# A two-layer hybrid trunk on one core: each GLA head's diagonal and smallest-block products come one projection product later, and layer 0's output projection takes K in another order

## The chip, the cores and the metric

The kernel runs on one core of a Trainium2 chip. The metric is the device time of one execution in microseconds, the median of several runs. A core has five engines with instruction streams of their own that meet only at semaphores: TensorE (PE; its weight loads are shown as PEld), VectorE (DVE), ScalarE (ACT), GpSimd (POOL) and SyncE (SP), which here issues the large weight loads as DMAs. Each engine takes its instructions strictly in the order in which they stand in its stream.

## What is computed

Two decoder layers on 512 tokens of width 1024. Layer 0 mixes by sliding-window attention and a short gated convolution, layer 1 by gated linear attention (GLA). A convolution MLP and a gated embedding follow in each. The two places that the change touches:

```python
def _attn_conv_mixer(h, ...):                      # layer 0
    ...
    return jnp.concatenate([attn, conv], axis=-1) @ w_out      # K = 512 attention + 512 convolution

def _gla_chunked(q, k, v, log_a):                  # layer 1, four heads, chunks of 64
    def step(state, inp):
        ...
        decay = jnp.exp(jnp.where(causal[:, :, None], rel, -jnp.inf))
        scores = jnp.einsum('bhtd,bhsd,bhtsd->bhts', qi, ki, decay)
        o_intra = jnp.einsum('bhts,bhsv->bhtv', scores, vi)
        state = jnp.exp(g_end)[..., None] * state + jnp.einsum(
            'bhsd,bhsv->bhdv', ki * jnp.exp(g_end[:, :, None, :] - gi), vi)
        return state, o_inter + o_intra
```

## The kernel before

Activations lie with features on the 128 partitions and the 512 tokens along the free axis. Almost all the work is products in fp32 precision made of three products of split operands (`mm3`, lines 157 to 159): the high half of the weight times the high half of the activation, high times low, low times high. Each weight block is loaded by SP into a buffer "raw" (two of them), ACT rounds it to the high half "wh" (line 137) and DVE subtracts that to make the low half "wl" (line 138).

**Layer 0's output projection** (`project`, line 348, with the `load` of line 745) goes through four blocks of 256 output columns. In each it loads all 1024 rows of K, and each of two output tiles sums 8 K tiles, 24 products. The K tiles are `ya + yc`: four attention tiles first, written by `mix` (line 640; its product is line 647, and ACT and DVE split it at lines 101 and 102), then four convolution tiles, of which `conv_out(0)` made two much earlier and `conv_out(1)` the other two just before. The attention rows of the weight are loaded by two DMAs for 64 partitions each, the convolution rows by one.

**GLA's heads** (`mixer1`, line 1472). While TensorE runs the layer's input projections (queries, keys, values and gates, in fp32r products of three), the intra-chunk scores of the four heads are worked out between them. A score block of 128x128 is cut into levels: at level b the lower-left blocks of b tokens in blocks of 2b are a product of two factors that carry the decay to the middle of the block. For each head h:

- `base(h)`: the running sum G of the log decays (DVE scan, line 1603); the factor of the diagonal, k times q at even tokens (line 1610); the sum over features of that factor by a product with ones (TensorE, line 1612); its placing on the even diagonal of the scores "sc" (DVE, line 1614, which reads the product from PSUM).
- `decay(h, levels)`: for each level, two differences of G (lines 1627, 1629), the exponential on ACT (1630; 1632 and 1633 at level 64) and the products with k and q (1634, 1635). `lo` is levels 64, 32, 16 and 8, `hi` is level 4.
- `level(h, levels)`: the products (lines 1648 and 1651) and their placing in sc (1659, 1661).
- `decay_pairs(h)` and `level_pairs(h)`: levels 2 and 1, with factors made in place in k and q (line 1676 on DVE, line 1678 on ACT), one set of products (1686) and four masked copies by DVE (1692, 1697).
- `decay_off`, `off`, `state`, `read`, `turn`: the part between chunks (transposes at 1730, states at 1743 and 1745), the output (1766, 1768, 1770, 1775) and its transposes (1782, 1786).

`query`, `key` and `gate` (lines 1520, 1526, 1531) are one projection product each, 24 products of 128x512. `Values.step(i)` is half of a value projection, 48 products of 128x336, whose sums ACT writes to vt (line 1505). The order of these calls at the end of `mixer1` (lines 1789 to 1889) is written out by hand; within it a scheduler places each engine's instructions, by priorities that follow the order of the calls.

Four PSUM buffers "ps" hold projection sums and four "pa" all other products. SBUF tiles with the tag "F" (the diagonal's factor, the levels' factors, the states' factors) share eight slots.

Of the kernel before, what the change touches and what calls it, by code (L numbers as in the profile page):

```python
# [18 lines left out]
P = 128  # L19
S = 512  # L20
# [36 lines left out]
class Kernel:  # L57
# [366 lines left out]
    def mixer0(self):  # L424
        nc, a, tc = self.nc, self.a, self.tc
        with tc.tile_pool(name="m0", bufs=1) as mp:
# [68 lines left out]
            h = HD // 2  # L495
# [161 lines left out]
            yc = [None] * 4  # L657
# [87 lines left out]
        def load(raw, cols):  # L745
            w = a["hy_w_out"][0]
            for g in range(2):
                nc.sync.dma_start(
                    raw[64 * g : 64 * g + 64, :4, :],
                    w[256 * g : 256 * g + 256, cols].rearrange("(j p) n -> p j n", p=64),  # L750
                )
            nc.sync.dma_start(raw[:, 4:, :], w[512:, cols].rearrange("(k p) n -> p k n", p=P))

        return lambda done, then: self.project(load, ya + yc, done, then)


    def operand(self, m, gain, tags):
# [714 lines left out]
    def mixer1(self):  # L1472
# [4 lines left out]
        with tc.tile_pool(name="m1", bufs=1) as mp:  # L1477
# [31 lines left out]
            def pair_w(c0):  # L1509
                return self.weights(w_in[:, :, c0 : c0 + 256], ND, 256)  # L1510
# [7 lines left out]
            def query(w, h):  # L1518
                o = qT[h] = self.fp.tile([P, S], F32, tag="a0", name=self.nm("qT"))
                nc.vector.scalar_tensor_tensor(  # L1520
                    out=o, in0=feature(w, h % 2), scalar=float(GDK**-0.5), in1=R, op0=ALU.mult, op1=ALU.mult
                )

            def key(w, h):
                o = kT[h] = self.fp.tile([P, S], F32, tag="a0", name=self.nm("kT"))
                nc.vector.tensor_tensor(o, feature(w, h % 2), R, ALU.mult)
# [70 lines left out]
            second = lambda x, b: x.rearrange("p (n b) -> p n b", b=2 * b)[:, :, b:]  # L1597
            scores, Gs, Fs = {}, {}, {}

            def base(h):  # L1600

                G = Gs[h] = mp.tile([P, S], F32, tag="G", name=self.nm("G"), bufs=2)
                nc.vector.tensor_tensor_scan(
                    G, run.rearrange("p a b -> p (a b)"), las[h], 0.0, op0=ALU.mult, op1=ALU.add
                )
                sc = scores[h] = mp.tile([P, GDV * NT], F32, tag="sc", name=self.nm("sc"), bufs=3)

                pr = new()[:, : S // 2]
                ev = lambda x: x.rearrange("p (n b) -> p n b", b=2)[:, :, 0]
                nc.vector.tensor_tensor(pr, ev(kT[h]), ev(qT[h]), ALU.mult)  # L1610
                pd = self.pa()[:, : S // 2]
                mm(pd, self.ones, pr, start=True, stop=True)
                nc.gpsimd.memset(sc[:, :S], 0.0)
                nc.vector.tensor_tensor(
                    sc[:, :S].rearrange("p (a n b) -> p a n b", a=NT, b=2)[:, :, :, 0],
                    pd.rearrange("p (a n) -> p a n", a=NT),
                    ev(self.ident).unsqueeze(1).to_broadcast([P, NT, P // 2]), ALU.mult,
                )
# [18 lines left out]
            def level(h, levels):  # L1637
                A = scores[h][:, :S]
                for l in levels:
                    b, F = LEVELS[l], Fs[h, l]  # L1640
                    pl = self.pa()
                    for t in range(NT):
                        c = slice(t * P, (t + 1) * P)
                        if b < 64:

                            for u in (0, 64):
                                d = slice(t * P + u, t * P + u + 64)
                                mm(second(pl[u : u + 64, d], b), F[:, d], second(F[:, d], b), start=True, stop=True)
                        else:
                            mid = t * P + b  # L1650
                            mm(pl[:b, mid : mid + b], F[:, t * P : mid], F[:, mid : mid + b], start=True, stop=True)
                    if b < 64:
                        for u in (0, 64):
                            r = slice(u, u + 64)
                            tv = lambda x: x.rearrange("p (t c) -> p t c", c=P)[r, :, r].rearrange(
                                "p t (n b) -> p t n b", b=2 * b
                            )[:, :, :, b:]
                            mk = second(msk[r, l, r], b).unsqueeze(1).to_broadcast([64, NT, 32 // b, b])
                            nc.vector.copy_predicated(tv(A), mk, tv(pl))
                    else:  # L1660
                        nc.vector.tensor_copy(second(A[:b], b), second(pl[:b], b))
# [18 lines left out]
            def level_pairs(h):  # L1680

                A = scores[h][:, :S]
                pl = self.pa()
                for d0 in range(0, S, 64):
                    d, u = slice(d0, d0 + 64), d0 % P
                    mm(pl[u : u + 64, d], kT[h][:, d], qT[h][:, d], start=True, stop=True)
                two, one = LEVELS.index(2), LEVELS.index(1)
                for u in (0, 64):
                    r = slice(u, u + 64)
                    v4 = lambda x: x.rearrange("p (t c) -> p t c", c=P)[r, :, r].rearrange("p t (n b) -> p t n b", b=4)  # L1690
                    m = msk[r, two, r].rearrange("p (n b) -> p n b", b=4)[:, :, 2:]
                    nc.vector.copy_predicated(
                        v4(A)[:, :, :, 2:], m.unsqueeze(1).to_broadcast([64, NT, 16, 2]), v4(pl)[:, :, :, 0:4:2]
                    )
                    v2 = lambda x: x.rearrange("p (t c) -> p t c", c=P)[r, :, r].rearrange("p t (n b) -> p t n b", b=2)
                    m = msk[r, one, r].rearrange("p (n b) -> p n b", b=2)[:, :, 1]
                    nc.vector.copy_predicated(
                        v2(A)[:, :, :, 1], m.unsqueeze(1).to_broadcast([64, NT, 32]), v2(pl)[:, :, :, 1]
                    )
# [111 lines left out]
            base(0)  # L1811
            decay(0, lo)
            query(w, 2)
            level(0, lo)
            decay(0, hi)
            decay_off(0)
# [1 line left out]
            query(w, 3)  # L1818
            w = pair_w(768)
            level(0, hi)  # L1820
            level_pairs(0)
            off(0)
            base(1)
            decay(1, lo)
            key(w, 2)
            key(w, 3)
            v = Values(0, 336, 336)
            level(1, lo)
# [2 lines left out]
            decay_pairs(1)  # L1831
            v.step(0)
            level(1, hi)
            level_pairs(1)
            off(1)
            base(2)
            decay(2, lo)
            v.step(1)
            v = Values(336, 672, 336)
            state(0)  # L1840
            level(2, lo)
            read(0)
# [2 lines left out]
            decay_pairs(2)  # L1845
            v.step(0)
            level(2, hi)
            level_pairs(2)
            off(2)
            turn(0)  # L1850
            base(3)
            decay(3, lo)
            v.step(1)
            w = pair_w(2064)
            state(1)
            level(3, lo)
            read(1)
# [7 lines left out]
            w = pair_w(2064 + 256)  # L1865
            self.load_vectors_ffn(1)
            level(3, hi)
            level_pairs(3)
            off(3)
            read(2)  # L1870
            gate(w, 2)
            turn(2)
            state(3)
# [54 lines left out]
```

## Time and profile before

| what | value |
|---|---|
| median of 3 runs | 1230.61 us (1229.55 to 1232.44) |
| the profiled execution | 1231.84 us |
| its span in the trace | 1230.1 us |
| TensorE's granted clock, mean | 0.999 |
| HBM traffic | 114.37 MB read, 2.10 MB written |

Line numbers (L137) are those of the kernel before. A row of the timeline gives start, duration, engine, line, operation, what it writes and reads, how many follow each other, and in brackets how long the engine sat idle before it and what ended that. Matmuls are pipelined: one starts before the one ahead of it has ended, so durations overlap and a wait is better measured from start to start. A row of the chain of waits gives start, duration and instruction. A row of the windows gives the stretch, its length, the busy time and number of instructions of PE, PEld, DVE, ACT and POOL, the clock, the busy share of the DMA engines and GB/s. A row of TensorE's waits gives what waited for whom, the total in us, how many times and the longest.

### The profile page before, as it was taken

What the parts mean: (1) busy time and instruction counts of PE and PEld (TensorE: products, weight loads), DVE (VectorE), ACT (ScalarE), POOL (GpSimd) and SP (SyncE); (2) the same over time, 40 slices, a digit from 0 to 9 for tenths busy, and PEclk for the clock granted to TensorE, in tenths of its full rate; (3) what the DMA queues carried; (4) which work ended last, traced back from release to release, by engine and by line L of the source; (5) the groups of instructions that cost most, each with busy time, mean ns of one, the idle gap of its engine ahead of it and who ended that gap; (6) DMA issues with size and microseconds to landing.
All of it is one profiled execution on the core that took longest, in us unless ns stands there. A gap on an engine that the chain in (4) does not pass through costs nothing.

```text
span 1230.1 us, 17710 instructions
## 1 busy us (share of the span) xinstructions
PE 1218.1 (99%) x7028; PEld 1053.8 (86%) x7028; DVE 969.7 (79%) x1537; ACT 665.7 (54%) x1084; POOL 43.7 (4%) x64
## 2 busy tenths in 40 slices
PE   9999999999999999999999999999999999999998
PEld 8877789989899889888987888889998989889887
DVE  6886587899898986746679875677999888987595
ACT  7466455656555644534563554555555555645374
POOL 2500000000000000000100000000000000000000
PEclk9999999999999999999999999999999999999999
DMA  7221322423233232222322222313242322422501
GB/s 217 87 88 46 86 78 69 137 69 116 91 103 103 93 130 95 94 91 88 112 91 68 70 69 69 103 42 130 69 137 69 121 85 95 146 95 95 205 2 69
DMA packets 111063, 117.61 MB, mean 96 GB/s; under 512 B 2776, under 2 KB 106258, under 8 KB 110980
## 3 DMA queue, kind: packets, MB, share of 16 engines
q1 hardware_dynamic: 109616, 115.35, 28.4%
q8 instruction: 55, 0.90, 0.3%
q0 software_dynamic: 560, 0.42, 0.3%
q10 hardware_dynamic: 804, 0.70, 0.2%
q14 instruction: 28, 0.23, 0.1%
HBM read 114.37 MB, written 2.10 MB: 95 GB/s over the span
## 4 chain that ended last, share of the span: by engine, by line
PE 79%; DVE 13%; ACT 3%; issue 2%; DMA 1%; POOL 1%; ACTq 0%; DVEq 0%; POOLq 0%
PE ps L157 12%; PE ps L158 11%; PE ps L159 11%; PE pa L158 6%; PE pa L157 6%; PE pa L159 6%; PE ps L847 5%; PE ps L845 5%; PE ps L846 5%; PE pa L847 2%; PE pa L846 2%; PE pa L845 2%; DVE wl L138 2%; DVE zt L905 1%; DMA raw<-in_ffn_w_up_dram 1%
## 5 line engine op out<-in xcount | busy, mean ns | idle before, releaser
L137 ACT ACTIVATE wh<-raw 128x1024 fp32r<-128x1024 f32 (+4 forms) x154 | 152.2, 991 | 159.0 <-PE ps L158 114.3
L138 DVE TENSOR_TENSOR wl<-raw,wh 128x1024 fp32r<-128x1024 f32 (+4 forms) x154 | 175.3, 1139 | 50.6 <-ACT wh L137 48.6
L793 ACT ACTIVATE wh<-raw 128x1024 fp32r<-128x1024 f32 x78 | 82.3, 1056 | 114.0 <-DVE raw L818 66.1
L905 DVE SCALAR_TENSOR_TENSOR zt<-z,vfa,zt 128x510 f32<-128x510 f32 (+1 forms) x176 | 131.2, 747 | 9.6 <-ACT zt L903 8.9
L794 DVE TENSOR_TENSOR wl<-raw,wh 128x1024 fp32r<-128x1024 f32 x78 | 95.4, 1223 | 14.8 <-ACT wh L793 14.7
L903 ACT ACTIVATE zt<-z,vfb 128x512 f32<-128x512 f32 x88 | 70.6, 809 | 16.4 <-DVE z L896 4.9
L157 PE MATMUL ps<-b,wh 128*128 128x512 f32 x192 | 76.2, 398 | 0.7 <-ACT b L101 0.5
L159 PE MATMUL ps<-b,wl 128*128 128x512 f32 x192 | 75.9, 396 | 0.0
L158 PE MATMUL ps<-b,wh 128*128 128x512 f32 x192 | 75.1, 392 | 0.0
L157 PE MATMUL pa<-a,wh 128*128 128x512 f32 x176 | 69.0, 392 | 0.0
L157 PE MATMUL pa<-b,wh 128*128 128x512 f32 x176 | 69.0, 392 | 0.0
L158 PE MATMUL pa<-a,wh 128*128 128x512 f32 x176 | 69.0, 392 | 0.0
L158 PE MATMUL pa<-b,wh 128*128 128x512 f32 x176 | 69.0, 392 | 0.0
L159 PE MATMUL pa<-a,wl 128*128 128x512 f32 x176 | 68.6, 390 | 0.1
L159 PE MATMUL pa<-b,wl 128*128 128x512 f32 x176 | 68.5, 389 | 0.0
L847 PE MATMUL ps<-four,wl 128*128 128x256 f32 x232 | 65.7, 283 | 0.0
L846 PE MATMUL ps<-four,wh 128*128 128x256 f32 x232 | 65.6, 283 | 0.0
L845 PE MATMUL ps<-four,wh 128*128 128x256 f32 x232 | 65.6, 283 | 0.0
L157 PE MATMUL ps<-a,wh 128*128 128x512 f32 x160 | 63.1, 394 | 0.0
L158 PE MATMUL ps<-a,wh 128*128 128x512 f32 x160 | 62.5, 391 | 0.0
L159 PE MATMUL ps<-a,wl 128*128 128x512 f32 x160 | 62.4, 390 | 0.0
L157 PE MATMUL ps<-uh,wh 128*128 128x512 f32 x128 | 50.3, 393 | 0.0
(470 smaller groups left out, 3527.4 us busy)
## 6 DMA issues: line engine op xcount, KB each, us to landing
raw<-in_ffn_w_up_dram SPq DMA_DIRECT2D x44, 1024.0 KB, 5.0
raw<-in_ffn_w_down_dram SPq DMA_DIRECT2D x13, 1024.0 KB, 4.7
raw<-in_hy_w_in_dram SPq DMA_DIRECT2D x8, 1024.0 KB, 4.9
raw<-in_gla_w_in_dram SPq DMA_DIRECT2D x8, 1024.0 KB, 5.1
raw<-in_ffn_w_down_dram SPq DMA_DIRECT2D x8, 768.0 KB, 4.3
raw<-in_ple_w_gate_dram SPq DMA_DIRECT2D x6, 1024.0 KB, 4.6
raw<-in_gla_w_out_dram SPq DMA_DIRECT2D x4, 1024.0 KB, 4.7
zt<-in_ffn_w_down_dram SPq DMA_DIRECT2D x6, 512.0 KB, 3.4
```

Source lines behind the costliest of these rows:

```text
L137: nc.scalar.activation(hv, v, AF.Copy)
L138: nc.vector.tensor_tensor(lv, v, hv.bitcast(F32), ALU.subtract)
L157: mm(out, lh, rh, start=start, stop=False, **kw)
L158: mm(out, lh, rl, start=False, stop=False, **kw)
L159: mm(out, ll, rh, start=False, stop=stop, **kw)
L793: nc.scalar.activation(h, src, AF.Copy)
L794: nc.vector.tensor_tensor(l, src, h.bitcast(F32), ALU.subtract)
L845: mm(out, wh, xh, start=first and j == 0, stop=False, **kw)
L846: mm(out, wh, xl, start=False, stop=False, **kw)
L847: mm(out, wl, xh, start=False, stop=j == ND // 2 - 1, **kw)
L903: nc.scalar.activation(y, z, AF.Identity, scale=w2[:, f : f + 1], bias=bb[:, f : f + 1])
L905: nc.vector.scalar_tensor_tensor(out=y[:, tap:], in0=z[:, : S - tap], scalar=w[:, f : f + 1], in1=y[:, tap:], op0=ALU.mult, op1=ALU.add,)
```

## The change

Two edits. First, in layer 0's output projection the order over K becomes convolution tiles 0 and 1, attention tiles 0 to 3, convolution tiles 2 and 3. The weight rows go to the matching places of the buffer, and the convolution rows come in two DMAs instead of one:

```diff
                 nc.sync.dma_start(
-                    raw[64 * g : 64 * g + 64, :4, :],
+                    raw[64 * g : 64 * g + 64, 2:6, :],
                     w[256 * g : 256 * g + 256, cols].rearrange("(j p) n -> p j n", p=64),
                 )
-            nc.sync.dma_start(raw[:, 4:, :], w[512:, cols].rearrange("(k p) n -> p k n", p=P))
-
-        return lambda done, then: self.project(load, ya + yc, done, then)
+            for k, r in ((0, 512), (6, 768)):
+                nc.sync.dma_start(raw[:, k : k + 2, :], w[r : r + 256, cols].rearrange("(k p) n -> p k n", p=P))
+
+
+        ys = yc[:2] + ya + yc[2:]
+        return lambda done, then: self.project(load, ys, done, then)
```

Second, `base(h)` keeps the scan, the diagonal's factor and the clearing of sc, and its product with ones and the placing become a function `diag(h)`, called one projection product later. `level_pairs(h)` is called one projection product later too:

```diff
-                pr = new()[:, : S // 2]
-                ev = lambda x: x.rearrange("p (n b) -> p n b", b=2)[:, :, 0]
+                pr = Fs[h, "diag"] = new()[:, : S // 2]
                 nc.vector.tensor_tensor(pr, ev(kT[h]), ev(qT[h]), ALU.mult)
+                nc.gpsimd.memset(sc[:, :S], 0.0)
+
+            def diag(h):
+                sc = scores[h]
                 pd = self.pa()[:, : S // 2]
-                mm(pd, self.ones, pr, start=True, stop=True)
-                nc.gpsimd.memset(sc[:, :S], 0.0)
+                mm(pd, self.ones, Fs[h, "diag"], start=True, stop=True)
                 nc.vector.tensor_tensor(
...
             query(w, 2)
+            diag(0)
             level(0, lo)
...
             level(0, hi)
-            level_pairs(0)
             off(0)
             base(1)
             decay(1, lo)
             key(w, 2)
+            level_pairs(0)
+            diag(1)
             key(w, 3)
...
             level(1, hi)
-            level_pairs(1)
             off(1)
             base(2)
             decay(2, lo)
             v.step(1)
             v = Values(336, 672, 336)
+            level_pairs(1)
+            diag(2)
             state(0)
...
             level(2, hi)
-            level_pairs(2)
             off(2)
             turn(0)
             base(3)
             decay(3, lo)
             v.step(1)
             w = pair_w(2064)
+            level_pairs(2)
+            diag(3)
             state(1)
...
             level(3, hi)
-            level_pairs(3)
             off(3)
             read(2)
+            level_pairs(3)
             gate(w, 2)
```

The number of instructions on TensorE, DVE, ACT and POOL stays the same; SP issues four DMAs more.

More of the change, by code (lines that the diff above doesn't have):

```diff
@@ L1598, in mixer1 @@
             scores, Gs, Fs = {}, {}, {}
+            ev = lambda x: x.rearrange("p (n b) -> p n b", b=2)[:, :, 0]
             def base(h):
```

## The prediction

> **What bounds the kernel now.** I read the page first, then TensorE's waits, the chain of waits and the two stages that the diff touches.
>
> ```profile
> span 1230.1 us, 17710 instructions
> ...
> PE 1218.1 (99%) x7028; PEld 1053.8 (86%) x7028; DVE 969.7 (79%) x1537; ACT 665.7 (54%) x1084; POOL 43.7 (4%) x64
> ```
> ```profile
> PE pa L1612 <- DVE F L1610: 1.5, 2, 1.0
> PE pa L1686 <- ACT qT L1678: 1.3, 2, 0.7
> ...
> PE ps L157 <- ACT b L101: 0.5, 1, 0.5
> ```
>
> TensorE is busy for 1218.1 of 1230.1 us, so the kernel is a string of products and an edit that adds or drops none can gain only where TensorE stands still: 12.0 us in all. Of its waits the diff aims at three: the diagonal product (L1612) for its factor from DVE, the smallest-block products (L1686) for qT from ACT, and layer 0's output projection (L157) for a split by ACT. Two things follow. The gain is a few us at most, and it holds only if no other engine is the limit in that place. That needs the windows and the chain in the GLA heads.
>
> ```profile
> 630.00:684.00 54.00, 51.50 (x403) 43.97 (x401) 52.68 (x126) 24.20 (x46) 0.00 (x0) 1.00 0.17 52
> ```
> ```profile
> 630.05 1.23 DVE wl L138
> ...
> 681.54 0.34 DVE F L1629
> ```
>
> From 630 to 684 us (columns: PE, weight loads, DVE, ACT, POOL) DVE is busy for 52.68 of 54.00 us, more than PE's 51.50, and the chain of work that ended last runs along DVE from 630.05 to 681.54, with one ACT step in between. So in heads 0 to 2 DVE sets the pace, and this change takes no DVE work away. It lets TensorE do other products meanwhile. The gain is the sum of TensorE's waits that vanish less those that DVE brings back elsewhere. The clock column is 1.00: it plays no part.
>
> **Part 1, layer 0's output projection.** All its products are kept; the order over K becomes two convolution tiles, the four attention tiles, the other two convolution tiles.
>
> ```profile
> 138.02 1.94 PE L647 MATMUL pa<-pT,v 128*64 128x512 f32 x8
> 140.43 0.98 PE L157 MATMUL ps<-b,wh 128*128 128x512 f32 x3 [0.46 <-ACT b L101]
> ...
> 142.63 0.40 PE L157 MATMUL ps<-b,wh 128*128 128x512 f32 x1
> ```
> ```profile
> 140.12 0.26 ACT L101 ACTIVATE b<-pa 128x128 fp32r<-128x128 f32 x1
> ...
> 142.35 0.28 ACT L101 ACTIVATE b<-pa 128x128 fp32r<-128x128 f32 x1 [0.36 <-DVE b L102]
> ```
> ```profile
> 142.66 0.29 DVE L102 TENSOR_TENSOR b<-pa,b 128x128 fp32r<-128x128 f32 x1 [0.34 <-ACT b L101]
> ```
>
> The attention product ends at 139.96 and the projection waits 0.46 us for the first split. A product of 0.39 us is followed after 0.227 (24 of them in 5.45), so 0.16 us of overlap is lost too. The nine products from 140.43 to 142.63 take 2.20 where nine at 0.227 take 2.04: another 0.16. The two convolution tiles were ready long before, so the whole **0.8 us** goes. Their six products take 1.36 us and end near 141.0; the attention splits run from 140.12 to 142.95, each needed 0.68 us after the one before, and the last low half (142.95) is needed near 143.2. That is a margin of 0.2 to 0.3. If the splits come later than that, the wait comes back there: 0 to 0.8 us.
>
> The weight load becomes four transfers instead of three (a 512 KB one is split), so SP's queue gets four more issues, one in each load; behind them stand only later weight loads, which wait for their buffers. POOL's queue keeps its order.
>
> ```profile
> raw<-in_hy_w_out_dram SPq DMA_DIRECT2D x8, 256.0 KB, 3.8
> raw<-in_hy_w_out_dram SPq DMA_DIRECT2D x4, 512.0 KB, 5.0
> ```
> ```profile
> 146.76 1.06 ACT L137 ACTIVATE wh<-raw 128x1024 fp32r<-128x1024 f32 x1 [4.12 <-PE ps L158]
> ```
>
> ACT starts on the next block at 146.76 because TensorE frees a buffer, not because data land, and it had stood idle for 4.12 us. Four more issues, one to each of the four loads, hide there: nothing. Without that cover each could cost at most its own 3.8 us. The Trainium skill (DMA: Bandwidth & Descriptors, Rules for kernel authors) speaks against this piece: it wants transfers of 1 MiB or more and advises against splitting. Its fit of about 2.0 us fixed cost for each would make an estimated 8 us for four loads if they were on the path; by the wait above they are not, and the measured 3.8 and 5.0 us decide.
>
> **Part 2, the heads.** Each head's L1612 (with its DVE reader L1614) and L1686 (with two L1692 and two L1697) move behind one more projection product. Every fp32 product is two rows of the trace. On DVE the four copies (about 0.45 us each, 1.8) now come after the next head's scan (L1603) and factor (L1610), which so start 1.8 us sooner; the copies' reader, the head's read, comes many us later. The last head's L1686 goes in among the products of read(2); it waited for nothing and I cost that move at nothing.
>
> ```profile
> 648.25 0.66 PE L1648 MATMUL pa<-F 128*64 128x32 f32 x16
> 649.53 0.69 PE L1686 MATMUL pa<-qT,kT 128*64 128x64 f32 x16 [0.61 <-ACT qT L1678]
> ...
> 654.19 0.67 PE L1612 MATMUL pa<-F,ones 128*128 128x256 f32 x2 [0.98 <-DVE F L1610]
> ...
> 672.73 0.66 PE L1648 MATMUL pa<-F 128*64 128x32 f32 x16
> 674.12 0.69 PE L1686 MATMUL pa<-qT,kT 128*64 128x64 f32 x16 [0.73 <-ACT qT L1678]
> ...
> 683.12 0.60 PE L1743 MATMUL pa<-vt,F 128*128 128x256 f32 x2
> 683.89 0.70 PE L1743 MATMUL pa<-vt,F 128*128 128x256 f32 x2 [0.17 <-ACT vt L1505]
> ...
> 698.72 0.66 PE L1648 MATMUL pa<-F 128*64 128x32 f32 x16
> 699.20 0.66 PE L1686 MATMUL pa<-qT,kT 128*64 128x64 f32 x16
> ...
> 702.98 0.67 PE L1612 MATMUL pa<-F,ones 128*128 128x256 f32 x2 [0.53 <-DVE F L1610]
> ```
>
> Undisturbed, L1686 starts 0.48 us after L1648 (698.72 to 699.20). In head 0 it took 1.28, in head 1 1.39: **0.80** and **0.91** us lost. The diagonals of heads 1 and 3 lose **0.98** and **0.53**; those of heads 0 and 2 wait for nothing. In head 2 the moved products also fill the **0.17** that L1743 waits for vt. Together 3.39 us; with part 1, 4.19.
>
> The Trainium skill (Trainium Kernel Development and Optimization, Performance Expectations) calls matmul busy time a bad metric, since matmuls are pipelined. By idle time alone, 0.61 and 0.73 in place of 0.80 and 0.91 and 0.46 in place of 0.8, the sum would be 0.71 less; I go by starts, as these rows allow.
>
> What comes back, **head 0**: the diagonal now stands right before the level products. PSUM's "pa" has four buffers, and diagonal, levels 64, 32, 16 and 8 need five, so the fifth waits until L1614 has read the diagonal. In the changed instruction lists L1614 stands behind qT's L1520.
>
> ```profile
> 641.09 1.57 PE L1648 MATMUL pa<-F 128*64 128x32 f32 x47
> ```
> ```profile
> 636.99 0.42 DVE L1614 TENSOR_TENSOR sc<-pa,cf 128x256 f32<-128x256 f32 x1
> 637.32 0.42 DVE L1629 TENSOR_TENSOR F<-G 128x256 f32<-128x256 f32 x1
> ...
> 642.28 0.70 DVE L1520 SCALAR_TENSOR_TENSOR qT<-ps,R 128x512 f32<-128x512 f32 x1
> 642.88 0.42 DVE L1661 COPY sc<-pa 64x256 f32<-64x256 f32 x1
> ```
>
> Taking L1614 and one more 0.33 us instruction away ahead of L1520 and putting one of 0.27 there brings L1520 to 641.9 and L1614 to 642.5, done at 642.9. TensorE reaches the last third of these rows at 641.09 + 2/3 of 1.5 = 642.1. So it waits about **0.85** us, and the level products, query(3) and SP's later loads stand behind it. Bounds: 0, and 1.7 if L1614 comes twice as late.
>
> **Head 1** has DVE's whole load behind it, so what TensorE wins must not run into it. The nearest place is the fourth "ps" bank of the value product, which key(3)'s L1526 frees:
>
> ```profile
> 664.58 0.67 DVE L1526 TENSOR_TENSOR kT<-ps,R 128x512 f32<-128x512 f32 x1
> ```
> ```profile
> 666.65 0.32 PE L157 MATMUL ps<-wh,b 128*128 128x336 f32 x1
> ```
>
> TensorE comes there at 666.65 less 0.80 and 0.98 plus 0.85: 665.72. DVE's order up to there holds the same instructions, so the bank is free at 665.25 as before: nothing, with 0.5 us to spare. Without head 0's wait it would come at 664.87 and lose **0.4**.
>
> **Heads 2 and 3**: the factor F keeps its slot until the diagonal, there are eight slots, and in the changed lists DVE's L1627 of the fourth level waits for that product, with all of DVE's queue behind it.
>
> ```profile
> 676.69 0.45 DVE L1692 COPY_PREDICATED sc<-msk,pa 64x128 f32<-64x128 uint8 x1
> 677.17 0.43 DVE L1627 TENSOR_TENSOR F<-G 128x256 f32<-128x256 f32 x1
> ...
> 682.46 0.86 DVE L138 TENSOR_TENSOR wl<-raw,wh 128x672 fp32r<-128x672 f32 x1
> 683.23 0.42 DVE L1634 TENSOR_TENSOR F<-F,kT 128x256 f32<-128x256 f32 x1
> 683.56 0.42 DVE L1635 TENSOR_TENSOR F<-F,qT 128x256 f32<-128x256 f32 x1
> ```
>
> In head 2, from the end of L1686, DVE has L1692, L1697, L1627, L1629, L138, L1634, L1635, L1692, L1614 before the first level product may write: three at 0.46, one at 0.77, five at 0.34 and about 0.2 of signals, 4.05 us. TensorE has the diagonal (0.6), three L1743 (six rows, about 0.28 each by 683.12's pair: 1.7) and eleven products of 128x336 at about 0.15 (1.7): 4.0. About **0** is left; 4.05 if the cover failed. In head 3 the DVE chain has no L138, L1634 or L1635 (2.5), and TensorE has diagonal, L1743 and two 128x512 products (2.8): **0**, or 2.5 without cover.
>
> **Sum.** 4.19 - 0.85 = 3.3 us. On the profiled execution's own time, 1231.84 us (span 1230.1 and 1.7 around it): 1228.5. It lies 1.2 above the median of the runs, 1230.61; on that scale **1227.3 us**.
>
> **Rivals.**
> - *Head 0 pays nothing.* L1614 is done in time, and only head 1's 0.4 comes back: 3.8 us, 1226.8. For it: ACT and DVE orders are only followed, their starts can slip forward. Against: the DVE window has 1.3 us free in 54.
> - *DVE is the limit and keeps it.* What vanishes in 630 to 684 (0.80, 0.98, 0.91, 0.17) reappears as waits for DVE, and only part 1 and head 3 stay, 0.8 + 0.53: 1229.3. For it: the chain on DVE. Against: the filling products of 128x336 are there, and each one done early counts.
> - *The projection's wait only moves* to the first attention split: 0.8 less gain, 1228.1. Against: 0.2 to 0.3 us of margin; for it: a margin that small.
> - *Slower: the F slot.* DVE stops at L1627 until the diagonal is done and the level products stand bare behind the chain, in head 2 for 4.05 and in head 3 for 2.5 us. 6.55 - 3.3 = 3.25 slower, 1233.9. It decides once TensorE's cover (4.0 and 2.8) doesn't run, as when the state products wait for vt or the early step products for their split weights.
>
> **How the numbers follow.** Chances: forecast 0.45, head 0 free 0.15, DVE keeps it 0.20, wait moves 0.07, slot 0.13. A difference under 0.2% (2.5 us) can't be told from none, so faster is below 1228.15, slower above 1233.07. The forecast, with about 1 us on either side, is faster in 0.39 of its 0.45 and same in 0.06; with head 0 free (0.15) and half of the moved wait (0.04) faster has 0.58. Same: 0.06 + 0.20 + 0.03 = 0.29. Slower: 0.13. The range goes from 1225.2 (all 4.19 us gone, 1226.4, and 1.2 for what lay between the profiled execution and the median) to 1230.8 (DVE keeps it, 1229.3, and 1.5 of a part-way slot wait) and leaves out the slot case in full and little below.
>
> **What would show it.** Right: in the after trace no wait of TensorE between L647 and L157; L1686 and L1612 without idle time in heads 0 to 3; L1648 in head 0 waiting 0.5 to 1 us for DVE's L1614; TensorE's busy time unchanged within 1 us; TensorE's idle time near 12.0 - 3.5 + 0.85 = 9.4 us. Wrong: L1651 or L1648 of heads 2 and 3 waiting over 1 us for DVE, L158 of the projection waiting for L102, or DVE idle at L1627 with TensorE idle in the same stretch.

## The result and the profile after

| what | before | after |
|---|---|---|
| median of 20 runs each | 1230.47 us | 1228.16 us |
| range | 1229.55 to 1232.44 | 1226.70 to 1229.34 |
| ratio, with its 95% interval | | 0.9981 (0.9974 to 0.9988) |
| the profiled execution, and its span | 1231.84, 1230.1 us | 1228.92, 1227.1 us |

The change makes the kernel 2.3 us faster (1.5 to 3.2 by the interval). The prediction was 1227.3 us, 3.3 under the median shown ahead of it, with a range from 1225.2 to 1230.8. Its own line for "faster", 1228.15, is missed by 0.01 us: it took 0.2% for what can't be told from no difference, but the interval of the ratio here lies wholly under 1. In the kernel after, line numbers are shifted: the diagonal's product and its placing are L1620 and L1621 (L1612, L1614 before), the level products L1655 and L1658 (L1648, L1651), the smallest blocks L1693 (L1686), the states L1750 (L1743), the output transposes L1789 (L1782), qT's scaling L1523 (L1520).

The page of the kernel after, its span and busy times, and then its view of TensorE's waits (who waited for whom, total, times, longest):

```profile
span 1227.1 us, 17714 instructions
...
PE 1217.1 (99%) x7028; PEld 1053.4 (86%) x7028; DVE 970.1 (79%) x1537; ACT 665.0 (54%) x1084; POOL 44.2 (4%) x64
```
```profile
PE pa L1655 <- DVE sc L1621: 1.1, 1, 1.1
PE ps L850 <- DVE t L797: 1.0, 2, 0.5
...
PE pa L159 <- DVE wl L138: 0.4, 1, 0.4
...
PE pa L1658 <- DVE sc L1621: 0.2, 1, 0.2
```

The three waits that the diff aims at (L157 for L101, L1612, L1686) are gone from the list, and the predicted new one stands there, L1655 for L1621. Busy time fell by 1.0 us, idle time from 12.0 to 10.0. The two FFN entries (L850, L159) come up again below.

**Where the time went, by stretches.** The change moves fp32 products between the projection products, but the projection rows (L157 to L159) keep their order, so the same projection row can be found in each trace. I cut the heads at three equal distances from one of them: 0, 132, 270 and 390 projection rows on. The stretches hold, in this order, head 0 with the diagonal of head 1 (227 product rows); the rest of head 1 and head 2 up to its level 8 (307); and the end of head 2 with head 3 (306). Each holds the same products before and after. In the tables they are called head 0, heads 1 and 2, and head 3. The windows between these rows (length, then busy time and instructions of PE, PEld, DVE, ACT and POOL, clock, DMA share, GB/s), of the kernel before:

```profile
625.04:661.96 36.92, 35.31 (x228) 28.55 (x227) 34.03 (x78) 19.24 (x31) 0.00 (x0) 1.00 0.13 38
661.96:696.93 34.97, 34.08 (x308) 30.74 (x307) 30.56 (x79) 15.85 (x38) 1.12 (x1) 1.00 0.23 70
696.93:738.66 41.73, 41.06 (x308) 34.56 (x307) 30.89 (x73) 22.44 (x51) 2.40 (x3) 1.00 0.24 77
```

and of the kernel after:

```profile
623.22:659.51 36.29, 35.14 (x229) 28.73 (x227) 33.40 (x77) 18.99 (x31) 0.00 (x0) 1.00 0.13 39
659.51:692.70 33.19, 33.05 (x308) 30.67 (x307) 30.44 (x78) 16.25 (x39) 1.11 (x1) 1.00 0.25 74
692.70:734.82 42.12, 41.83 (x308) 34.81 (x307) 31.90 (x74) 21.89 (x50) 2.76 (x3) 1.00 0.25 76
```

The three lengths change by -0.63, -1.78 and +0.39, together **2.02 us** less. Length less busy time is TensorE's idle time: 1.61, 0.89 and 0.67 before, 1.15, 0.14 and 0.29 after. So idle time explains 1.59 of the 2.02; in the second stretch 1.03 us went out of "busy" rows, and in the third 0.77 came into them. Idle time alone would have missed both.

**The projection.** TensorE's timeline of the kernel after:

```profile
137.18 1.94 PE L647 MATMUL pa<-pT,v 128*64 128x512 f32 x8
139.06 0.50 PE L157 MATMUL ps<-b,wh 128*128 128x512 f32 x1
...
140.56 0.39 PE L157 MATMUL ps<-b,wh 128*128 128x512 f32 x1
```

From the start of the attention product to the projection's first product it takes 1.88 us by these rows, before 2.41 (138.02 to 140.43): **0.53** gone, and no split is waited for afterwards.

These two, 2.55 us, are what the edits do in the places that they touch. What else lies between the two profiled executions differs from run to run, as the last experiments show, but for one small thing: from the end of DVE's last TENSOR_TENSOR to the end of the span it takes 3.05 us before and 2.81 after. Of the kernels in the experiments, every one with three transfers in a load has the first figure and every one with four the second, within 0.01. No run shows why.

### The profile page after: what moved, and what is told of

It is laid out like the page before. It is cut to its first block, busy times and chain, and to the rows that moved or that the text cites. A ratio compares the mean times of both kernels' runs of the same rounds, so it can differ in the third digit from the quotient of the medians.

```text
span 1227.1 us, 17714 instructions
## 1 busy us (share of the span) xinstructions
PE 1217.1 (99%) x7028; PEld 1053.4 (86%) x7028; DVE 970.1 (79%) x1537; ACT 665.0 (54%) x1084; POOL 44.2 (4%) x64
## 4 chain that ended last, share of the span: by engine, by line
PE 83%; DVE 10%; ACT 2%; issue 2%; DMA 2%; POOL 1%; DVEq 0%; ACTq 0%; POOLq 0%
PE ps L157 13%; PE ps L158 12%; PE ps L159 12%; PE pa L158 6%; PE pa L157 6%; PE pa L159 6%; PE ps L850 5%; PE ps L848 5%; PE ps L849 5%; PE pa L850 2%; PE pa L849 2%; PE pa L848 2%; DMA raw<-in_ffn_w_up_dram 2%; DVE wl L138 1%; DVE wl L797 1%
## 5 line engine op out<-in xcount | busy, mean ns | idle before, releaser
L138 DVE TENSOR_TENSOR wl<-raw,wh 128x1024 fp32r<-128x1024 f32 (+4 forms) x154 | 175.2, 1139 | 50.5 <-ACT wh L137 48.9
L797 DVE TENSOR_TENSOR wl<-raw,wh 128x1024 fp32r<-128x1024 f32 x78 | 95.4, 1223 | 14.5 <-ACT wh L796 14.4
L157 PE MATMUL ps<-b,wh 128*128 128x512 f32 x192 | 76.8, 400 | 0.0
L159 PE MATMUL ps<-b,wl 128*128 128x512 f32 x192 | 75.7, 394 | 0.0
L159 PE MATMUL pa<-b,wl 128*128 128x512 f32 x176 | 68.7, 390 | 0.4 <-DVE wl L138 0.4
L157 PE MATMUL pa<-b,wh 128*128 128x512 f32 x176 | 69.0, 392 | 0.0
L157 PE MATMUL pa<-a,wh 128*128 128x512 f32 x176 | 69.0, 392 | 0.0
L159 PE MATMUL pa<-a,wl 128*128 128x512 f32 x176 | 68.6, 390 | 0.0
L850 PE MATMUL ps<-four,wl 128*128 128x256 f32 x232 | 65.7, 283 | 0.0
L157 PE MATMUL ps<-a,wh 128*128 128x512 f32 x160 | 63.1, 394 | 0.0
L159 PE MATMUL ps<-a,wl 128*128 128x512 f32 x160 | 62.4, 390 | 0.0
L157 PE MATMUL ps<-uh,wh 128*128 128x512 f32 x128 | 50.3, 393 | 0.0
```

The source lines that it names most:

```text
L138: nc.vector.tensor_tensor(lv, v, hv.bitcast(F32), ALU.subtract)
L157: mm(out, lh, rh, start=start, stop=False, **kw)
L159: mm(out, ll, rh, start=False, stop=stop, **kw)
L797: nc.vector.tensor_tensor(l, src, h.bitcast(F32), ALU.subtract)
L850: mm(out, wl, xh, start=False, stop=j == ND // 2 - 1, **kw)
```

## The experiments

All times are beside runs of the kernel before on the same chip. The stretches of every profile, and the median against the kernel before (negative is faster):

| kernel | projection | head 0 | heads 1, 2 | head 3 | the three, against before | median against before |
|---|---|---|---|---|---|---|
| before | 2.41 | 36.92 | 34.97 | 41.73 | | |
| before, second profile | 2.41 | 36.92 | 34.95 | 41.77 | +0.02 | |
| after | 1.87 | 36.29 | 33.19 | 42.12 | -2.02 | -2.31 |
| after, second profile | 1.87 | 36.29 | 33.17 | 42.14 | -2.02 | |
| new K order alone | 1.87 | 36.98 | 34.91 | 41.77 | +0.04 | -0.07 |
| the same, three transfers | 1.87 | 36.97 | 34.90 | 41.76 | +0.01 | -0.04 |
| heads alone | 2.41 | 36.29 | 33.17 | 42.14 | -2.02 | -1.31 |
| smallest blocks alone | 2.40 | 36.84 | 34.98 | 41.80 | 0.00 | +0.99 |
| diagonals alone | 2.41 | 36.02 | 35.14 | 41.92 | -0.54 | -0.26 |
| after, head 0's diagonal early | 1.87 | 35.28 | 33.78 | 42.16 | -2.40 | -3.19 |
| after, head 0's diagonal later | 1.87 | 34.95 | 34.04 | 42.10 | -2.53 | -2.06 |
| after, nine slots | 1.87 | 36.32 | 33.09 | 41.43 | -2.78 | -3.41 |
| nine slots, diagonal early | 1.87 | 35.26 | 34.13 | 41.46 | -2.77 | -3.15 |
| before, nine slots | 2.41 | 36.95 | 34.28 | 42.13 | -0.26 | -0.34 |

A stretch repeats within 0.04 us between two profiles of one kernel. Medians carry an interval of about 0.9 us on either side in the main comparison and 1.0 to 1.3 in the others, so below that I read the stretches and take the medians as a check.

### The two edits by themselves

The new K order alone is the kernel before with the diff's first edit. With three transfers, the load stays and the products take the tiles in the order 4, 5, 0, 1, 2, 3, 6, 7:

```diff
-                for k in range(ND):
-                    self.mm3(pss[c], w(k, c * P, (c + 1) * P), ks[k], start=k == 0, stop=k == ND - 1)
+                for n, k in enumerate(order):
+                    self.mm3(pss[c], w(k, c * P, (c + 1) * P), ks[k], start=n == 0, stop=n == ND - 1)
...
-        return lambda done, then: self.project(load, ya + yc, done, then)
+        return lambda done, then: self.project(load, ya + yc, done, then, (4, 5, 0, 1, 2, 3, 6, 7))
```

The heads alone are the kernel after with the old load and `ya + yc`.

> The old kernel with layer 0's output projection alone changed (new order over K, four weight transfers in each load). Theory: 0.8 us less than the old kernel (0.6 to 1.0), no wait of TensorE between L647 and L157, and no wait on the splits after it. Rival, the wait only moves: a wait of L157 or L158 for L101 or L102 of 0.5 us or more a little later, and the time is unchanged. Rival, the split weight load costs: up to 3.8 us more for each of three later blocks, seen as a wait of L158 for L137 or L138 in the stage from 144 to 163 us. The heads from 612 us on should show the old waits (0.98, 0.91, 0.80, 0.53 us).

> The old kernel with the new order over K alone; the weight load keeps its three transfers and its layout. Theory (the fourth transfer is free): the same time as with four transfers within 0.3 us, 0.6 to 1.0 us under the old kernel. Rival, each further transfer costs about 2 us of issue and set-up where it stands on the path: this run is faster than the one with four transfers by 1 us or more, and the stage from 144 to 163 us shows it.

> The changed kernel with layer 0's old load and old order over K: the heads' moves alone. Theory: 3.39 us of waits vanish and 1.15 us come back in head 0 (as the changed kernel's trace has it), so about 2.2 us less than the old kernel, and with the projection's own run about the whole change. TensorE's lead over the old kernel at 740 us about 2.3 us. If the weight loads of FFN layer 1 at 977 us land 0.9 us late because of the earlier heads, this run has the stalls of 0.80 and 0.76 us near 985 and 995 us too, and the gain ends near 1.2 us; if that landing is chance, they may be there or not, whichever kernel it is. Rival, DVE keeps it: lead at 740 us of 0.5 us.

Measured: 1230.23 us for the new order, 1230.26 with three transfers (before: 1230.30; ratios 0.9996, 0.9987 to 1.0005, and 0.9997, 0.9988 to 1.0005), 1228.99 with the heads alone (0.9989, 0.9980 to 0.9997). By the trace the order gains 0.53 and 0.54 us, under the 0.6 that I expected at least; the medians can't tell so little. The wait didn't move. The fourth transfer costs nothing: the two kernels' times and stretches are the same. The Trainium skill (DMA: Bandwidth & Descriptors, Rules for kernel authors) asks to make one large transfer of many small ones; going against that has no price here, where the load runs ahead of its use. The heads alone gain the same 2.02 as in the whole change, so the edits add.

### The two halves of the heads' edit

Both are the heads alone, with one half taken back. Smallest blocks alone, in each head as in these two:

```diff
             base(0)
+            diag(0)
             decay(0, lo)
             query(w, 2)
-            diag(0)
...
             base(1)
+            diag(1)
             decay(1, lo)
             key(w, 2)
             level_pairs(0)
-            diag(1)
```

Diagonals alone, in each head as in this one:

```diff
             level(0, hi)
+            level_pairs(0)
             off(0)
...
             key(w, 2)
-            level_pairs(0)
             diag(1)
```

> The old load and order in layer 0; in the heads only the smallest-block products are moved, each diagonal stands right behind its factor's making as before. Theory: 0.80 and 0.91 us vanish in heads 0 and 1, the diagonals keep their 0.98 and 0.53 us, and head 0 has no buffer wait since four products stand on four buffers: 1.7 us less than the old kernel (1.3 to 1.9). Rival, DVE keeps it: what vanishes at the smallest-block products comes back at the next product that waits for DVE within head 1, and the time is within 0.5 us of the old kernel's.

> The old load and order in layer 0; in the heads only the diagonals are moved, the smallest-block products stand behind the level products as before and keep their waits for qT (0.80 and 0.91 us). Theory: the diagonals' 0.98 and 0.53 us vanish, head 0's buffer wait of about 1.15 us comes, and may run together with the 0.80 us that the smallest-block products wait for qT, which is then hidden: 0.4 to 1.2 us less than the old kernel. Rival, head 0's buffer wait is not due to the diagonal's place: no wait of L1648 for L1614 there (old numbering), and 1.5 us less.

Measured: 1230.94 us (before 1229.95; 1.0008, 0.9999 to 1.0017) and 1229.69 (0.9998, 0.9989 to 1.0007). The first expectation failed altogether: of 1.7 us nothing came. The timeline of TensorE with the smallest blocks alone (L1617 is the diagonal there):

```profile
651.44 0.67 PE L1617 MATMUL pa<-F,ones 128*128 128x256 f32 x2 [1.34 <-DVE F L1611]
...
673.37 0.67 PE L1617 MATMUL pa<-F,ones 128*128 128x256 f32 x2 [0.37 <-DVE F L1611]
```

and with the diagonals alone (L1652 is a level product, L1690 the smallest blocks):

```profile
642.41 0.66 PE L1652 MATMUL pa<-F 128*64 128x32 f32 x16 [1.18 <-DVE sc L1618]
...
673.46 0.69 PE L1690 MATMUL pa<-qT,kT 128*64 128x64 f32 x16 [1.62 <-ACT qT L1682]
```

Where only the smallest blocks are moved away, TensorE comes to head 1's diagonal earlier and waits there 1.34 us instead of 0.98, and to head 2's 0.37 instead of nothing; in heads 1 and 2 the smallest blocks' own wait is gone and the length is still 34.98. Where only the diagonals are moved, the smallest blocks of head 1 wait 1.62 instead of 0.73. The two products hang on the same chain of DVE and ACT, and the one left in its place takes up part of what the other gains.

With the smallest blocks alone, that isn't all. In head 0 their 0.80 us are freed, the diagonal of head 1 takes 0.36 of them, and the stretch is only 0.08 shorter. The rest goes where the moved products now stand by themselves between two projection products (head 0, the smallest blocks alone):

```profile
655.27 0.69 PE L1690 MATMUL pa<-qT,kT 128*64 128x64 f32 x16
655.88 0.50 PE L157 MATMUL ps<-b,wh 128*128 128x512 f32 x1
656.22 0.39 PE L158 MATMUL ps<-b,wh 128*128 128x512 f32 x1
```

From the projection product ahead of them (654.95) to the second one behind (656.22) it takes 1.27 us, where the two take 0.45 without them: 0.82 us for products that cost about 0.50 behind those of level 4, in their old place. So of the 0.72 that are missing, 0.36 are waiting moved on and 0.32 the price of standing alone. In the kernel after they stand together with the diagonal: 1.25 us for both (653.68 to 655.38, less 0.45). The heads gain 0.00 and 0.54 us by the halves alone, 2.02 together.

### Head 0

The kernel after with the diagonal earlier:

```diff
             base(0)
+            diag(0)
             decay(0, lo)
             query(w, 2)
-            diag(0)
             level(0, lo)
```

and later:

```diff
             query(w, 2)
-            diag(0)
             level(0, lo)
...
             query(w, 3)
             w = pair_w(768)
+            diag(0)
             level(0, hi)
```

In the second the placing of the diagonal, which writes zeros into the rest of the even columns, comes after the first levels' copies and overwrites what they had put there: head 0's scores lack it, while every instruction still runs.

> The changed kernel with head 0's diagonal put back to its old place, before the projection product; all else as changed. Theory (five products on four buffers, L1614 of the old numbering late behind qT's L1520): the wait of 1.15 us of head 0's level products for the diagonal's reader is gone, and 0 to 0.4 us comes back in head 1 at the value product's fourth buffer: 0.75 to 1.15 us less than the changed kernel. Rival, DVE sets the pace in 630 to 684 us: the wait moves on into head 1 in full and the time is the changed kernel's within 0.3 us.

> The changed kernel with head 0's diagonal moved on, behind the projection product of query(3) in place of before the first level products. Theory (the fifth product on four buffers waits for the diagonal's reader): there are four products ahead of query(3) again, the wait of 1.15 us goes, and 0 to 0.4 us comes back in head 1: 0.75 to 1.15 us less than the changed kernel. Rival, the qT scaling on DVE is what the level products would wait for anyway, or DVE sets the pace: the wait shows at another product of 640 to 665 us with about the same length, and the time is the changed kernel's within 0.3 us.

Measured: 1227.11 us (0.9975, 0.9966 to 0.9985) and 1227.89 (0.9981, 0.9972 to 0.9989). First the kernel after, TensorE's timeline in head 0, then DVE's:

```profile
637.96 0.59 PE L1620 MATMUL pa<-F,ones 128*128 128x256 f32 x2
...
638.96 1.10 PE L1655 MATMUL pa<-F 128*64 128x32 f32 x31
641.21 0.66 PE L1655 MATMUL pa<-F 128*64 128x32 f32 x16 [1.15 <-DVE sc L1621]
```
```profile
640.04 0.70 DVE L1523 SCALAR_TENSOR_TENSOR qT<-ps,R 128x512 f32<-128x512 f32 x1
640.64 0.43 DVE L1621 TENSOR_TENSOR sc<-pa,cf 128x256 f32<-128x256 f32 x1
```

The level-8 products, the fifth user of four buffers, wait for L1621, and L1621 stands behind qT's scaling. With the diagonal at either other place this wait is gone, and head 0 is 1.01 and 1.34 us shorter. So its cause is the diagonal's place, as the count of five products on four buffers says; a fifth buffer itself was not tried. But heads 1 and 2 become 0.59 and 0.85 us longer, and 0.38 and 0.51 us are left, less than I expected at least. TensorE's timeline with the diagonal early:

```profile
664.07 0.42 PE L157 MATMUL ps<-wh,b 128*128 128x336 f32 x1 [0.34 <-DVE kT L1529]
```

It is the fourth "ps" bank, for which the prediction had named 0.4; with the diagonal later it is 0.58. Measured from start to start, this one place holds all that is given back: in the kernel after, the projection product ahead of this row and the row itself are each followed after 0.15 us (from 664.05 on); with the diagonal early they are followed after 0.66 and 0.26 (from 663.41), with the diagonal later after 0.90 and 0.26 (from 663.31).

### The slots of F

```diff
-            new = lambda: mp.tile([P, S], F32, tag="F", name=self.nm("F"), bufs=8)
+            new = lambda: mp.tile([P, S], F32, tag="F", name=self.nm("F"), bufs=9)
```

> The changed kernel with nine slots in place of eight for the factors F. Theory: in the changed kernel the slot cost nothing worth naming (0.16 us in head 3, none in head 2), so this kernel is within 0.4 us of the changed one; DVE does its fourth-level products earlier in heads 2 and 3 and no longer waits for the diagonal there. Rival, the slot holds DVE back and sets the pace of the following heads: 0.7 us or more faster than the changed kernel, with the gain in 680 to 740 us.

> The changed kernel with nine slots for the factors F and head 0's diagonal back in its old place. The two edits alone brought TensorE's rows after the heads 0.75 and 0.39 us ahead of the changed kernel's; theory: they act in different heads (3 and 0 to 1) and add, so the heads end 1.1 us ahead of the changed kernel's (0.8 to 1.2), no wait of the level products of head 0, and the time is 0.2 to 0.6 us under that with nine slots alone. Rival, what head 0 gains is taken back by DVE before head 2: the time of nine slots alone within 0.2 us.

> The old kernel with nine slots for the factors F, nothing else. In the changed kernel the ninth slot brought TensorE's rows behind head 3 another 0.75 us ahead. Theory: the shortage is of the change's own making, since a factor that waits for a later diagonal keeps its slot longer; here, with every diagonal read at once, the ninth slot gives less than 0.3 us in the heads, and the time is the old kernel's within 0.5 us. Rival: eight slots hold DVE back in either kernel, and this one ends the heads about 0.75 us earlier than the old kernel.

Measured: 1226.54 us (0.9971, 0.9961 to 0.9982), the lowest median of all; 1226.88 with the diagonal early too (0.9973, 0.9964 to 0.9983); 1229.85 for the kernel before with nine slots (0.9996, 0.9987 to 1.0005). For the first the rival held, by the stretches: the ninth slot shortens head 3 by 0.69 and heads 1 and 2 by 0.10. DVE's timeline in head 3, of the kernel after:

```profile
704.52 0.43 DVE L1699 COPY_PREDICATED sc<-msk,pa 64x128 f32<-64x128 uint8 x1 [1.99 <-PE pa L1693]
...
705.24 0.44 DVE L1634 TENSOR_TENSOR F<-G 128x256 f32<-128x256 f32 x1
...
717.18 1.66 DVE L1782 TENSOR_SCALAR sc<-pa,rq 128x256 f32<-128x256 f32 x4 [0.90 <-POOL rq L167]
```

and with nine slots:

```profile
699.98 0.41 DVE L1636 TENSOR_TENSOR F<-G 128x256 f32<-128x256 f32 x1
...
702.93 0.41 DVE L1642 TENSOR_TENSOR F<-F,qT 128x256 f32<-128x256 f32 x1
...
715.71 1.66 DVE L1782 TENSOR_SCALAR sc<-pa,rq 128x256 f32<-128x256 f32 x4 [0.90 <-POOL rq L167]
```

With eight slots L1634 needs the slot that the diagonal's factor holds, and stands behind the copies L1699; DVE is idle for 1.99 us and makes the level's factors, from L1634 on, only once TensorE has read the diagonal. With nine it has the last of them, L1642, done before 703.4. TensorE shows no idle row for that delay. It shows in rows that get longer, the transposes L1789 of what L1782 writes, first after, then nine slots:

```profile
717.87 1.79 PE L1789 MATMUL pa<-cf,sc 128*128 128x128 f32 x8
```
```profile
717.43 1.03 PE L1789 MATMUL pa<-cf,sc 128*128 128x128 f32 x8
```

The same eight products last 1.79 us where they begin 0.69 us after L1782 does, and follow it one by one, and 1.03 us where they begin 1.72 us after it: 0.76 us of waiting that is counted as busy. The kernel before had most of this too:

```profile
722.48 1.61 PE L1782 MATMUL pa<-cf,sc 128*128 128x128 f32 x8
```

So against the kernel before, the change costs 0.18 us here, and the ninth slot takes away 0.58 more that was there already. The Trainium skill (Trainium Kernel Development and Optimization, Performance Expectations) calls matmul busy time a bad metric for how close a kernel is to roofline, because matmuls are pipelined; these rows show one more way in which it misleads.

In the kernel before the ninth slot gives 0.26 us in the heads together. That is less than 0.3, as expected, but it doesn't show that the shortage is of the change's own making: heads 1 and 2 are 0.69 us shorter and head 3 is 0.40 longer. TensorE's timeline of that kernel in head 1, and a row of its waits:

```profile
672.17 0.66 PE L1648 MATMUL pa<-F 128*64 128x32 f32 x16
672.66 0.66 PE L1686 MATMUL pa<-qT,kT 128*64 128x64 f32 x16
```
```profile
PE pa L1743 <- ACT st L1750: 0.7, 1, 0.7
```

L1686 follows L1648 after 0.49 us. So the 0.91 us that head 1's smallest blocks lost, and that the prediction priced as a wait for qT, go with one more slot and no move at all, and the transposes take 1.03 us here as well. What takes most of it back is head 2's diagonal, which comes 0.26 us dearer, and in head 3 a state product that now waits 0.7 us for ACT, about 1.0 us by starts. Eight slots hold DVE back in both kernels; the places where TensorE pays for it differ.

And in the kernel after, with the diagonal early, the gains don't add: against nine slots alone head 0 is 1.06 us shorter, and heads 1 and 2 are 1.04 longer. TensorE's timeline of that kernel names what takes it back, a state product that waits for ACT, and a level product whose wait for DVE was 0.4 with nine slots alone:

```profile
680.68 0.70 PE L1750 MATMUL pa<-vt,F 128*128 128x256 f32 x2 [0.49 <-ACT st L1757]
682.46 0.59 PE L1658 MATMUL pa<-F 128*64 128x64 f32 x7 [0.77 <-DVE sc L1704]
```

### What differs from run to run

> The old kernel once more, unchanged. In its first profile TensorE's rows stall for 0.3 to 0.5 us more than usual at 248.8 and 258.9 us and at 998.7 us, in the two FFNs. Theory: these stalls come with the landing of weight loads and differ from run to run, so this profile has them at other places, longer or not at all, and its span differs from 1230.1 us by up to 1.5 us for that alone. Rival: they belong to the program, and stand at the same places with the same lengths. The waits of the heads (0.98, 0.91, 0.80, 0.53 us) and of the projection (0.46 us) are the same within 0.1 us either way.

> The changed kernel once more, unchanged. In its first profile TensorE stalls at 257.3, 985.2 and 995.6 us (about 0.55 us more than usual each), the last two behind a weight load that took 6.9 us. Theory: run to run, as for the old kernel, so other places or none, and the span may be up to 1.5 us shorter. Rival: the change has moved the loads so that they collide there every time, and the same stalls are here. Head 0's wait for the diagonal's reader is 1.15 us again, within 0.1.

Measured: one execution each, 1230.69 and 1227.14 us, spans 1228.9 and 1225.4. The heads' waits and stretches are the same as in the first profiles. The FFN stalls are not: the old kernel's three are gone, and of the changed kernel's three only the one near 257 us is there again, shorter. In FFN layer 1, ACT's timeline at the one weight load that comes late, before and after (first profiles):

```profile
986.55 1.06 ACT L137 ACTIVATE wh<-raw 128x1024 fp32r<-128x1024 f32 x1 [1.33 <-DMA raw<-in_ffn_w_up_dram]
```
```profile
983.60 1.06 ACT L137 ACTIVATE wh<-raw 128x1024 fp32r<-128x1024 f32 x1 [2.26 <-DMA raw<-in_ffn_w_up_dram]
```

In the second profiles this wait is 1.15 us before and 0.95 after, and TensorE shows no wait in this FFN. With 1.33 us TensorE waits 0.2 some 12 us later (before, L847 for L794); with 2.26 it waits 0.5 at the same product (L850 for L797), and 0.4 for L138 ahead of that. So the first profile of the kernel after holds 0.9 us of stalls here that its second profile, of the same program, hasn't. Whether such landings come more often in some of these kernels than in others, which could be why "smallest blocks alone" has a median 0.99 over before at equal stretches, stays open: one profile or two of each can't tell.

## Why the prediction was near, step by step

The sign and the mechanism held: waits of TensorE that are filled with other products, less one new wait in head 0. The edits are worth 2.55 us by the stretches where the sum said 3.3, and the median's 2.3 agrees with 2.55. The difference of 0.8 has four parts: 0.27, 0.30 and 0.92 us less than forecast, and 0.70 more. Together they are 2.2 us of error, so that the sum came so near is in part luck.

- **Part 1, 0.8 predicted, 0.53 measured.** "0.16 us of overlap" and "another 0.16" of slow rows were the mis-sized terms. The first six rows, of convolution tiles whose operands were ready long before, take 1.50 us (139.06 to 140.56) where six at 0.227 take 1.36: they aren't slow for the splits, and nine rows take 2.20 us as before. What goes is the idle time of 0.46 and 0.07 more.
- **The waits of head 0 and of head 1's diagonal, 0.80 and 0.98**, vanish. The new wait was put at 0.85 and is 1.15: L1621 came where the prediction had it (0.6 us behind qT's scaling), TensorE some 0.2 us earlier. 0.80 + 0.98 - 1.15 gives the measured 0.63.
- **Heads 1 and 2, 0.91 + 0.17 predicted, 1.78 measured.** The 0.17 was mis-sized: I took the flagged idle time of L1743 for the loss. TensorE's timeline before, and after:

```profile
683.89 0.70 PE L1743 MATMUL pa<-vt,F 128*128 128x256 f32 x2 [0.17 <-ACT vt L1505]
684.52 0.62 PE L1651 MATMUL pa<-F 128*64 128x64 f32 x7
...
685.45 0.70 PE L1743 MATMUL pa<-vt,F 128*128 128x256 f32 x2
686.08 0.42 PE L1648 MATMUL pa<-F 128*64 128x32 f32 x6
```
```profile
679.87 1.03 PE L1750 MATMUL pa<-vt,F 128*128 128x256 f32 x4
680.54 0.50 PE L157 MATMUL ps<-wh,b 128*128 128x336 f32 x1
680.92 0.70 PE L1750 MATMUL pa<-vt,F 128*128 128x256 f32 x2
681.27 0.50 PE L158 MATMUL ps<-wl,b 128*128 128x336 f32 x1
```

  Before, the three pairs take 0.77 (683.12 to 683.89), 0.63 and 0.63, together 2.03 us; after, four rows take 0.67 and two 0.35, 1.02. Here alone 1.01 us went, and with the 0.91 that is 0.14 more than the stretch gained. Of the 1.01 only 0.17 is a flagged wait; why each pair took longer before is not shown. And the 0.91 needed no move, as the ninth slot in the kernel before shows.
- **Head 3, 0.53 predicted as gain, 0.39 measured as loss.** The diagonal's wait is gone: up to the projection product ahead of the transposes (722.25 before, 717.64 after) the stretch is 0.38 us shorter. Two steps failed. One is "the last head's L1686 goes in among the products of read(2); ... I cost that move at nothing". Where it stood in one piece before, it stands in two after:

```profile
731.48 0.67 PE L1686 MATMUL pa<-qT,kT 128*64 128x64 f32 x16
732.07 0.55 PE L1730 MATMUL pa<-cf,F 128*128 128x128 f32 x3
```
```profile
728.63 0.59 PE L1775 MATMUL pa<-st,F 128*128 128x256 f32 x2
729.16 0.33 PE L1693 MATMUL pa<-qT,kT 128*64 128x64 f32 x2
729.42 0.70 PE L1773 MATMUL pa<-vt,sc 128*128 128x256 f32 x2
729.95 0.59 PE L1775 MATMUL pa<-st,F 128*128 128x256 f32 x2
730.48 0.68 PE L1693 MATMUL pa<-qT,kT 128*64 128x64 f32 x14
731.09 0.50 PE L158 MATMUL ps<-b,wh 128*128 128x512 f32 x1
```

  From its start to the next product it took 0.59; now it is 0.26 and 0.61, and each L1775 pair ahead of it takes 0.53, where such pairs took 0.43 before (733.41 to 733.84). That is 0.5 us, and 0.6 of loss by the starts of shared rows from there on (730.51 before, 726.08 after) to the end of the stretch. The other is "heads 2 and 3: the F slot ... 0". TensorE's cover did hold (the wait for L1621 there is 0.16 us), but DVE's delay reached TensorE later, at the transposes: 1.79 us where they took 1.61 before, 0.18 of loss. So 0.38 of gain and 0.6 and 0.18 of loss make the 0.39. The 0.76 us that a ninth slot gains there are mostly what the kernel before lost already.
- **The rivals.** "DVE keeps it" is in part what each half of the heads' edit shows alone, and not what the whole shows. "The slot" was right that DVE is delayed at that instruction and that this costs, and wrong in where and how much: no level product stands bare, and the transposes lose 0.18 us more than before, not 6.55. "Head 0 pays nothing" and "the wait moves" didn't come.

## What to carry to other kernels

Waits that hang on one chain of another engine can't be priced one by one: moving one of two products out of the way gained 0.00 or 0.54 us, moving both 2.02. Ask also where a moved group of small products will stand: alone between two projection products it cost 0.82 us, behind another group about 0.50. When a product's reader is put off, count the buffers that it now holds, in PSUM (1.15 us here) and in the factors' pool, and look for the price several steps later. And try the pool's size in the kernel before as well: only there did it show that the slots had cost 0.91 and 0.58 us already. Measure from start to start of rows that both orders share; idle time alone missed 1.03 us of gain in one stretch and 0.77 of loss in the next.

## What the runs showed of the hardware

Eight fp32 products 128x128 that each wait a little for DVE appear as 1.79 us of busy time without any idle row, where 1.03 is their undisturbed length. Sixteen fp32 products that stand alone between two projection products cost 0.82 us where behind another group they cost about 0.50. A stretch of 33 to 42 us of interleaved work repeats within 0.04 us from run to run, while one weight load of 1 MiB made ACT wait between 0.95 and 2.26 us for it, and TensorE 0 to 0.9 us.
